# First mixer: the last two heads' projections ahead of most of the attention's; adaLN in thirds of a place, four pieces in a row

## The chip, the cores and the metric

The kernel runs on one core of a Trainium2 chip. The metric is device microseconds of one execution, from the first instruction to the last; a kernel is judged by the median of several executions. TensorE is called PE in the rows (its weight loads PEld), VectorE DVE, ScalarE ACT, GpSimd POOL, and SyncE, which only issues transfers here, SP.

## The reference, cut to what matters

A network of four layers on one sequence of 256 tokens, width 1024, in float32:

```
for layer in (0, 1):                               # first block
    mix = even_mixer(h)  if layer == 0 else  odd_mixer(h)
    h = layer_norm(a * h + mix);   h = layer_norm(a * h + conv_ffn(h))
for i in (0, 1):                                   # second block, conditioned on one vector c
    shift, scale, gate = split(silu(c) @ ada_w[i, 0] + ada_b[i, 0])       # adaLN, a "place"
    y = stick_breaking_attention(h * (1 + scale) + shift)  or  retention(...)
    h = layer_norm(a * h + (1 + gate) * y)
    shift, scale, gate = split(silu(c) @ ada_w[i, 1] + ada_b[i, 1])
    h = layer_norm(a * h + (1 + gate) * grouped_moe(h * (1 + scale) + shift))
```

`even_mixer` projects x to six heads of a gated delta rule ("DeltaNet": a causal convolution, then for each head a triangular solve and a scan over chunks of 64, gated by a projection z) and to four heads of a dilated attention (q, k, v in three groups, softmax, weights times v). `odd_mixer` projects to four heads of differential attention and four of gated linear attention (GLA). The adaLN parameters depend on c alone: four places (i, j) of 3072 numbers each, a vector of 1024 times a matrix of 1024 x 3072, 48 MB of weights in all. Nothing needs them before the second block.

## The kernel before, in words

Tokens lie as two tiles t of 128. Each projection of the first block splits weights and activations into a high and a low part and multiplies three times (`mm3`, L402 to L404). The weights come in pieces of 1 MB through a ring of six buffers; SP issues the loads (L356) in program order, each as soon as its buffer is free. PE works strictly in program order; what that order is, is decided while the program is built.

`drive` builds it: it takes one step of each active chain in turn (a chain runs in a slot; chains of one slot come one after the other) and after each the next step of a filler. In the mixers the filler is a list of items, each a generator with a condition; `work` takes the first item whose condition holds.

In `even_mixer` (items at L980 to L988) the items are `head_proj(0)`, (2), (4), which project q, k, v of two DeltaNet heads each; `swa_qk` (six) and `swa_v` (three), the attention's projections; and `z_proj(0)`, (2), (4). `z_proj(4)` waits for the flag ("pe", 0), the end of the first pair of heads. The chains are one `gdn_head` for each DeltaNet head in two slots (start L1077, inverse by levels L1151, L1158, L1159 with a masked copy L1162 on DVE, tail L1170 to L1189), eight attention units `swa_unit(h, t)` in one slot (scores L931, scale and bias L934 to L942 on DVE, softmax L819 to L821, transposes L831, weights times v L952, normalised L954), and `pair_end`, which norms and gates two heads and transposes them (L498). The attention units need all of `swa_v`. `outproj_ln` follows: L402 to L404 with 512 columns, then a layer norm whose last step is ACT L707.

The adaLN work is `ada(n)` (L1474 to L1508): n pieces of a queue of 48. A piece is one 1 MB load of 256 columns (8 row blocks), eight products of the vector with it (L1496: the vector is broadcast to 32 columns and each product goes to one of four column groups of the array), a copy to SBUF on ACT (adasb, L1502), two products with a selecting vector that sum the groups and turn the row into columns (`finish`, L1483), and two bias adds on ACT (L1486, tile adac). `N_ADA` = (18, 17, 3, 0): 18 pieces in the even mixer, one after every second item; 17 in the odd; 3 in each of three `build_xT` (transposes L423, affine L446, split L436), ahead of its first token tile; `ada(48)` (L2264) does what is left, four, ahead of the second block.

Of the kernel before, what the change touches and what calls it, by code (L numbers as in the profile page):

```python
# [15 lines left out]
AF = mybir.ActivationFunctionType  # L16
ALU = mybir.AluOpType
# [4 lines left out]
P = 128  # L22
S = 256
NT = S // P
D = 1024
KD = D // P
# [17 lines left out]
N_ADA = (18, 17, 3, 0)  # L44
# [6 lines left out]
def _consts():  # L51
    f = np.float32
    k = np.arange(P)[:, None]
    i = np.arange(P)[None, :]
    parts = {}
# [6 lines left out]
    parts["sel"] = (np.arange(P)[:, None] % 32 == 0)  # L62
    parts["MBpos"] = np.where(i <= k, 0.0, BIG)
    parts["MBneg"] = np.where(i >= k, 0.0, -BIG)
    c = np.arange(2 * P)[None, :]
# [52 lines left out]
class Net:  # L118
# [448 lines left out]
    def init_cols(self, r):  # L567


        nc = self.nc  # L570
        ps = self.bank()
# [12 lines left out]
        self.adaq = [(i, c) for i in range(4) for c in range(12)]  # L584
# [251 lines left out]
    def even_mixer(self, xn, n_ada=0):  # L836
        nc, T, tc = self.nc, self.T, self.tc
# [4 lines left out]
        with tc.tile_pool(name="em", bufs=2) as gp, self.psum_phase(c0=2, c1=2, x=1) as self.pc:  # L842
# [116 lines left out]
            def pair_end(hp):  # L959
# [18 lines left out]
            fl = self.flags  # L978
# [4 lines left out]
                *[(None, lambda i=i, b=b: swa_qk(i, b)) for b in (0, 2, 4) for i in range(2)],  # L983
                *[(None, lambda g=g: swa_v(g)) for g in range(GRP)],
                (lambda: {("go", 2), ("go", 3)} <= fl, lambda: head_proj(4)),
# [16 lines left out]
            for i in range(n_ada):  # L1002
                items.insert(4 + 2 * i, (None, lambda: self.ada(1)))
# [212 lines left out]
    def odd_mixer(self, x, xn, n_ada=0):  # L1216
# [6 lines left out]
        with tc.tile_pool(name="om", bufs=2) as op, self.psum_phase(d0=1, d1=1, g=3) as self.pc:  # L1223
# [239 lines left out]
            for i in range(n_ada):  # L1463
                items.insert(min(len(items), 3 + 2 * i), (None, lambda: self.ada(1)))
# [11 lines left out]
    def ada(self, n):  # L1476

        nc = self.nc
        prev = None

        def finish(i, c, ps, sb):
            for j in range(2):
                nc.tensor.matmul(ps[:, 256 + j : 257 + j], sb[:, j * P : j * P + P], self.sel, start=True, stop=True)  # L1483
            for j in range(2):
                dst = self.adac[:, i, 2 * c + j : 2 * c + j + 1]
                nc.scalar.activation(dst, ps[:, 256 + j : 257 + j], AF.Identity, bias=dst)  # L1486

        for _ in range(min(n, len(self.adaq))):
            i, c = self.adaq.pop(0)
            w = self.T["ada_w_2"][i // 2, i % 2].rearrange("(k p) c -> p k c", p=P)  # L1490
            wi = self.wload(w[:, :, c * 256 : c * 256 + 256], [P, KD, 256])
            wt = self.wtile(wi)
            ps = self.bank()
            for k in range(KD):
                q = (k % 4) * 32
                nc.tensor.matmul(ps[q : q + 32, :256], self.adas[:, k : k + 1].to_broadcast([P, 32]),  # L1496
                                 wt[:, k, :], start=k < 4, stop=k >= 4, tile_position=(0, q))
            yield
            if prev:
                finish(*prev)  # L1500
            sb = self.lp.tile([P, 256], F32, tag="adasb", bufs=2, name=self.nm("adasb"))
            nc.scalar.activation(sb, ps[:, :256], AF.Copy)  # L1502
            prev = (i, c, ps, sb)
            yield
        if prev:
            yield
            finish(*prev)
# [797 lines left out]
```

## Time and profile before

| | us |
|---|---|
| runs | 1894.43, 1890.86, 1882.28 |
| median of the three | 1890.86 |
| profiled execution | 1891.04 |
| its span | 1889.0 |
| PE busy in it | 1749.1 (93%) |
| even mixer, to its first output product | 0 to 282.72 |
| its output projection | 282.72 to 307.73 |
| build 1 and first FFN | 307.73 to 513.88 |
| build 2 and odd mixer with its output projection | 513.88 to 692.33 |
| build 3 and second FFN | 692.33 to about 896.7 |

Each stage ends where the next one's first PE instruction starts. In the rows of the trace a line is the start in us, the busy time, engine, line, operation, out<-in by the program's names with shapes, and in brackets how long the engine was idle ahead of it and what released it. A product in float32 is two passes, so a line's count is twice that of the program's instructions. Neighbouring products overlap, so the spacing of starts, not the busy time, is what one costs in a full stretch.

### The profile page before, as it was taken

To read this page: it belongs to the slowest core of one execution; us is meant where nothing else is said; L and a number is where in the kernel's file an instruction comes from. 1 tells how busy PE (TensorE), PEld (TensorE's weight loads), DVE (VectorE), ACT (ScalarE), POOL (GpSimd) and SP (SyncE) were. 2 spreads that over 40 slices of the span, in tenths; PEclk is the share of its full clock that TensorE was granted. 3 is DMA by queue.
4 is the path that set the end of the run, shared out by engine and by line. 5 is a ranking of instruction groups with operands and counts; after the bars stand their busy time and mean duration, and the time that the engine had idled before them with its cause. 6 is when DMAs were issued, how large, how long until landed. Compare 5 with 4: busy or idle time off the path is not lost. (4 is left out here: it accounts for less than half of the span.)

```text
span 1889.0 us, 29304 instructions
## 1 busy us (share of the span) xinstructions
PE 1749.1 (93%) x11781; PEld 1345.5 (71%) x11781; DVE 1040.1 (55%) x1963; ACT 711.4 (38%) x1346; POOL 230.5 (12%) x275
## 2 busy tenths in 40 slices
PE   7999998999989989999799799999689997999995
PEld 6989876999878869999698444433589985444432
DVE  6865854877767558777655532111477655422113
ACT  5444434555465455555565211111334332111111
POOL 2121201000043111000300010000133420100002
PEclk9999998999989989999899799999799998999998
DMA  8455554455566674556534899997344459799980
GB/s 272 149 168 164 161 175 156 157 201 197 162 212 213 210 269 157 188 172 198 186 135 166 328 401 397 401 400 265 102 149 136 155 208 348 297 402 400 403 322 24
DMA packets 275367, 434.85 MB, mean 230 GB/s; under 512 B 10549, under 2 KB 176007, under 8 KB 275093
## 3 DMA queue, kind: packets, MB, share of 16 engines
q1 hardware_dynamic: 271828, 428.49, 64.2%
q0 software_dynamic: 2016, 2.49, 0.5%
q8 instruction: 97, 1.59, 0.3%
q10 hardware_dynamic: 1377, 1.88, 0.3%
q14 instruction: 49, 0.40, 0.1%
HBM read 431.77 MB, written 1.05 MB: 229 GB/s over the span
## 5 line engine op out<-in xcount | busy, mean ns | idle before, releaser
L270 DVE TENSOR_TENSOR wl<-w,wh 128x1024 fp32r<-128x1024 f32 (+1 forms) x312 | 388.1, 1244 | 199.0 <-ACT wh L269 197.9
L269 ACT ACTIVATE wh<-w 128x1024 fp32r<-128x1024 f32 (+1 forms) x312 | 328.7, 1055 | 365.9 <-PE ps L403 175.5
L402 PE MATMUL ps<-xh,wh 128*128 128x256 f32 (+1 forms) x1312 | 384.9, 294 | 9.3 <-ACT xh L436 8.0
L403 PE MATMUL ps<-xl,wh 128*128 128x256 f32 (+1 forms) x1312 | 376.2, 287 | 0.0
L404 PE MATMUL ps<-xh,wl 128*128 128x256 f32 (+1 forms) x1312 | 375.2, 286 | 0.5 <-DVE wl L270 0.5
L402 PEld LDWEIGHTS ps<-xh,wh 128*128 128x128 f32 (+1 forms) x1312 | 253.2, 193 | 17.0 <-ACT xh L436 8.3
L403 PEld LDWEIGHTS ps<-xl,wh 128*128 128x128 f32 (+1 forms) x1312 | 253.4, 193 | 3.2 <-issue 0.8
L404 PEld LDWEIGHTS ps<-xh,wl 128*128 128x128 f32 (+1 forms) x1312 | 252.9, 193 | 2.4 <-DVE wl L270 1.0
L402 PE MATMUL ps<-wh,xh 128*128 128x256 f32 x512 | 155.6, 305 | 1.8 <-DVE rvg L728 1.4
L404 PE MATMUL ps<-wh,xl 128*128 128x256 f32 x512 | 148.3, 290 | 1.0 <-DVE xl L437 1.0
L403 PE MATMUL ps<-wl,xh 128*128 128x256 f32 x512 | 149.0, 291 | 0.0
L402 PE MATMUL pc<-wh,yh 128*128 128x512 f32 x336 | 132.1, 397 | 1.0 <-DVE yl L270 0.9
L403 PE MATMUL pc<-wl,yh 128*128 128x512 f32 x336 | 132.9, 395 | 0.0
L404 PE MATMUL pc<-wh,yl 128*128 128x512 f32 x336 | 131.6, 393 | 0.4 <-DVE yl L270 0.3
L2074 PE MATMUL pc<-w,xs 128*64 128x512 f32 x512 | 121.8, 595 | 0.0
L2074 PE MATMUL ps<-w,xs 128*64 128x512 f32 x512 | 113.3, 595 | 0.9 <-ACT pt L264 0.9
L402 PEld LDWEIGHTS ps<-wh,xh 128*128 128x128 f32 x512 | 101.5, 198 | 5.7 <-issue 2.2
L404 PEld LDWEIGHTS ps<-wh,xl 128*128 128x128 f32 x512 | 101.0, 197 | 2.0 <-DVE xl L437 1.8
L403 PEld LDWEIGHTS ps<-wl,xh 128*128 128x128 f32 x512 | 101.8, 199 | 0.4 <-issue 0.2
L2035 PEld LDWEIGHTS ps<-pe,x 128*128 128x128 f32 x576 | 70.5, 201 | 27.3 <-issue 24.3
L2074 PEld LDWEIGHTS pc<-w,xs 128*64 128x64 f32 x512 | 37.3, 137 | 72.7 <-issue 70.2
L2085 PE MATMUL ps<-w,hT 128*64 128x512 f32 x256 | 85.8, 595 | 0.0
(550 smaller groups left out, 2619.4 us busy)
## 6 DMA issues: line engine op xcount, KB each, us to landing
w<-in_moe_w_gate_dram SPq DMA_DIRECT2D x68, 1024.0 KB, 13.7
w<-in_moe_w_up_dram SPq DMA_DIRECT2D x68, 1024.0 KB, 14.7
w<-in_moe_w_down_dram SPq DMA_DIRECT2D x68, 1024.0 KB, 14.0
w<-in_ada_w_dram SPq DMA_DIRECT2D x48, 1024.0 KB, 5.9
w<-in_ffn_w_up_dram SPq DMA_DIRECT2D x44, 1024.0 KB, 5.3
w<-in_ret_w_in_dram SPq DMA_DIRECT2D x24, 1024.0 KB, 5.3
w<-in_ffn_w_down_dram SPq DMA_DIRECT2D x22, 1024.0 KB, 4.9
w<-in_w_in_even_dram SPq DMA_DIRECT2D x21, 1024.0 KB, 5.4
```

Source lines behind the costliest of these rows:

```text
L269: self.nc.scalar.activation(hi, src, AF.Copy)
L270: self.nc.vector.tensor_tensor(lo, src, hi.bitcast(F32), op=ALU.subtract)
L402: mm(ps, lh, rh, start=first, stop=False)
L403: mm(ps, lh, rl, start=False, stop=False)
L404: mm(ps, ll, rh, start=False, stop=last)
L2035: mm(ps[:, k * P : k * P + P], xn[:, t, (4 * a + k) * P : (4 * a + k + 1) * P], pef[:, t, :], start=t == 0, stop=t == 1)
L2074: mm(ps[64 * e : 64 * e + 64, :], xs[:, k, 64 * e : 64 * e + 64], wt[2 * (k // 4) + e][:, k % 4, :], start=k == 0, stop=k == KD - 1)
L2085: mm(ps[64 * e : 64 * e + 64, :], hT[:, f * P + 64 * e : f * P + 64 * e + 64], wt[2 * (f // 2) + e][:, f % 2, hf * 512 : hf * 512 + 512], ...
```

## The change

- `ada`: twelve pieces instead of 48. A piece is 1024 columns, a third of a place: four loads of 1 MB in a row (two row blocks of 1024 columns each, so that a row of a block is 4 KB in one run instead of 1 KB), 32 products (each row block against the four column quarters; quarter q goes to column group q), one copy of 128 x 256 to SBUF, two products with a selecting matrix of four columns, two adds on DVE. The products L1496 stay 384 and the bytes 48 MB; copies go from 48 to 12, finishing products from 96 to 24, adds from 96 on ACT to 24 on DVE.
- `N_ADA` = (4, 4, 1, 0): 16 MB in the even mixer (18 before), 16 in the odd (17), 4 in each build (3), 4 at the end (4).
- Even mixer: the four pieces stand behind all other items instead of between them. Since `z_proj(4)` waits for its flag, they come ahead of it.
- Odd mixer: a piece after every seventh item instead of every second; the last two follow all projections.
- `head_proj(4)` moves from behind `swa_v` to behind the first two `swa_qk`, with its old condition.

```diff
-N_ADA = (18, 17, 3, 0)
+N_ADA = (4, 4, 1, 0)
-    parts["sel"] = (np.arange(P)[:, None] % 32 == 0)
+    parts["sel"] = (k == 32 * np.arange(4)[None, :])
-        self.adaq = [(i, c) for i in range(4) for c in range(12)]
+        self.adaq = [(i, c) for i in range(4) for c in range(3)]
-                *[(None, lambda i=i, b=b: swa_qk(i, b)) for b in (0, 2, 4) for i in range(2)],
+                (None, lambda: swa_qk(0, 0)),
+                (None, lambda: swa_qk(1, 0)),
+                (lambda: {("go", 2), ("go", 3)} <= fl, lambda: head_proj(4)),
+                *[(None, lambda i=i, b=b: swa_qk(i, b)) for b in (2, 4) for i in range(2)],
                 *[(None, lambda g=g: swa_v(g)) for g in range(GRP)],
-                (lambda: {("go", 2), ("go", 3)} <= fl, lambda: head_proj(4)),
-                items.insert(4 + 2 * i, (None, lambda: self.ada(1)))
+                items.insert(len(items) - i, (None, lambda: self.ada(1)))
-                items.insert(min(len(items), 3 + 2 * i), (None, lambda: self.ada(1)))
+                items.insert(min(len(items), 3 + 7 * i), (None, lambda: self.ada(1)))
     def ada(self, n):
-            wi = self.wload(w[:, :, c * 256 : c * 256 + 256], [P, KD, 256])
+            ws = [self.wload(w[:, k : k + 2, c * D : c * D + D], [P, 2, D]) for k in range(0, KD, 2)]
             ps = self.bank()
             for k in range(KD):
-                q = (k % 4) * 32
-                nc.tensor.matmul(ps[q : q + 32, :256], self.adas[:, k : k + 1].to_broadcast([P, 32]),
-                                 wt[:, k, :], start=k < 4, stop=k >= 4, tile_position=(0, q))
+                for q in range(0, P, 32):
+                    nc.tensor.matmul(ps[q : q + 32, :256], self.adas[:, k : k + 1].to_broadcast([P, 32]),
+                                     self.wtile(ws[k // 2])[:, k % 2, 8 * q : 8 * q + 256],
+                                     start=k == 0, stop=k == KD - 1, tile_position=(0, q))
             yield
-            if prev:
-                finish(*prev)
             sb = self.lp.tile([P, 256], F32, tag="adasb", bufs=2, name=self.nm("adasb"))
             nc.scalar.activation(sb, ps[:, :256], AF.Copy)
-            prev = (i, c, ps, sb)
             yield
-        if prev:
             yield
-            finish(*prev)
+            for j in range(2):
+                nc.tensor.matmul(ps[:, 256 + 4 * j : 260 + 4 * j], sb[:, j * P : j * P + P], self.sel,
+                                 start=True, stop=True)
+            for j in range(2):
+                dst = self.adac[:, i, 8 * c + j : 8 * c + 8 : 2]
+                nc.vector.tensor_tensor(dst, ps[:, 256 + 4 * j : 260 + 4 * j], dst, op=ALU.add)
```

How the instructions now stand, at three places. First PE in the last part of the even mixer, from the last projection product of `z_proj(4)` on (gD and gW are the inverse of a DeltaNet head, ident,sc the attention's transposes, vb,spT its weights times v, w,adacc an adaLN product). Before, it begins:

```order
L404 MATMUL ps_2873<-wh_2697,xl_116 128x256
L1496 MATMUL ps_2976<-w_2742,adacc 32x256 x8
L1151 MATMUL pc_2987<-gD_2464,gna_2425 128x128 x2
L1151 MATMUL pc_2992<-gD_2765,gna_2710 128x128 x2
L1483 MATMUL ps_2976<-cst_171,adasb_2985 128x1 x2
L1496 MATMUL ps_3003<-w_2777,adacc 32x256 x8
L831 MATMUL pc_3013<-ident,sc_2860 128x128 x4
```

and after the change, from the first complete unit of tile 1 in it:

```order
L498 MATMUL ps_3013<-ident,gon_2019 128x128
L498 MATMUL ps_3020<-ident,gon_2019 128x128
L931 MATMUL pc_3028<-kb,qb 128x256 x2
L931 MATMUL pc_3032<-kb,qb 128x256
L831 MATMUL pc_3042<-ident,sc_3027 128x128 x4
L831 MATMUL pc_3048<-ident,sc_3027 128x128 x2
L952 MATMUL pc_3052<-vb,spT_3041 128x64 x6
L931 MATMUL pc_3065<-kb,qb 128x128 x3
```

Where the end of two heads and three adaLN pieces stood between the attention's instructions, the attention's instructions now follow one another. Behind the last projection there were 40 DeltaNet products, two and a half attention units, and three adaLN pieces; now there are 9 DeltaNet products, four units and a half, and 26 products of the adaLN piece of build 1, which belong to the last unit's waits.

Second, SP's loads ahead of that. Before, adaLN and projection weights alternate:

```order
L356 DMA w_1285<-in_ada_w_dram 128x8x256
L356 DMA w_1393<-in_w_in_even_dram 128x8x256
L356 DMA w_1424<-in_ada_w_dram 128x8x256
L356 DMA w_1538<-in_w_in_even_dram 128x8x256
L356 DMA w_1582<-in_ada_w_dram 128x8x256
```

and now sixteen adaLN loads stand in a row, of which these are the first with the last projection piece ahead of them:

```order
L356 DMA w_1517<-in_w_in_even_dram 128x8x256
L356 DMA w_1879<-in_ada_w_dram 128x2x1024
L356 DMA w_1978<-in_ada_w_dram 128x2x1024
L356 DMA w_2082<-in_ada_w_dram 128x2x1024
L356 DMA w_2189<-in_ada_w_dram 128x2x1024
L356 DMA w_2303<-in_ada_w_dram 128x2x1024
```

Only the weights of `z_proj(4)` and of the output projection come behind them.

Third, PE at the end of the odd mixer (glq,glk are the GLA scores of the last level, glv,gla_kn its state, gla_at its weights, gla_st,gla_qe the state's part of the output, ident,oo transposes of the heads' outputs). Before, from the last projection products on:

```order
L402 MATMUL ps_7065<-wh_6936,xh_5632 128x256
L403 MATMUL ps_7065<-wl_6937,xh_5632 128x256
L404 MATMUL ps_7065<-wh_6936,xl_5633 128x256
L1496 MATMUL ps_7159<-w_6818,adacc 32x256 x8
L1400 MATMUL pc_7174<-glv,gla_at 128x128
L1403 MATMUL pc_7174<-gla_st,gla_qe 128x128
```

and after the change, from the second adaLN piece behind the last projection on:

```order
L1489 MATMUL ps_6943<-w_6779,adacc 32x256 x8
L1444 MATMUL pc_6990<-dfv,dpT_6924 128x128
L1444 MATMUL pc_6999<-dfv,dpT_6929 128x128 x2
L1498 MATMUL ps_6943<-cst_171,adasb_6988 128x4 x2
L1365 MATMUL pc_7005<-glq,glk 128x128
L1365 MATMUL pc_7006<-glq,glk 128x128
```

The last projection product stood four heads' final GLA products ahead of the mixer's end, with seven adaLN pieces around and behind them; now it stands ahead of the last two levels of the GLA scores (L1365, before L1363), the state (L1391), all its outputs, and two adaLN pieces.

## Rows read from the trace of the kernel before

**Rows 1.** The page: span, and the adaLN loads (KB each, median us to landing).

```profile
span 1889.0 us, 29304 instructions
...
w<-in_ada_w_dram SPq DMA_DIRECT2D x48, 1024.0 KB, 5.9
```

**Rows 2.** PE in order of time, end of the last projection of the even mixer.

```profile
254.21 0.28 PE L404 MATMUL ps<-wh,xl 128*128 128x256 f32 x1
254.42 1.07 PE L1496 MATMUL ps<-w,adacc 128*32 128x256 f32 x16
255.42 1.16 PE L1151 MATMUL pc<-gD,gna 128*128 128x128 f32 x8
256.42 0.50 PE L1483 MATMUL ps<-cst,adasb 128*128 128x1 f32 x4
256.85 1.07 PE L1496 MATMUL ps<-w,adacc 128*32 128x256 f32 x16
```

**Rows 3.** PE in order of time, the attention's last units before the output projection.

```profile
263.21 1.45 PE L952 MATMUL pc<-vb,spT 128*128 128x64 f32 x12
...
265.99 0.93 PE L931 MATMUL pc<-kb,qb 64*128 64x128 f32 x6
...
270.90 0.79 PE L952 MATMUL pc<-vb,spT 128*128 128x64 f32 x6
...
272.23 1.13 PE L931 MATMUL pc<-kb,qb 64*128 64x256 f32 x4
...
277.79 0.60 PE L831 MATMUL pc<-ident,sc 128*128 128x128 f32 x4
...
280.09 2.12 PE L952 MATMUL pc<-vb,spT 128*128 128x64 f32 x12 [0.52 <-DVE spT L266]
...
282.72 0.77 PE L402 MATMUL pc<-wh,yh 128*128 128x512 f32 x1
```

**Rows 4.** Windows: PE, PEld, DVE, ACT, POOL busy (instructions), PEclk, DMA share, GB/s.

```profile
254.00:265.00 11.00, 11.00 (x120) 9.08 (x118) 5.69 (x12) 5.75 (x18) 0.00 (x0) 1.00 1.01 346
...
270.00:275.00 5.00, 4.62 (x28) 3.29 (x25) 2.70 (x9) 0.49 (x1) 0.00 (x0) 1.00 0.00 0
275.00:280.00 5.00, 2.97 (x18) 1.99 (x17) 2.88 (x9) 2.53 (x8) 0.00 (x0) 1.00 0.00 0
280.00:285.00 5.00, 4.53 (x21) 3.86 (x22) 2.65 (x10) 0.39 (x1) 1.03 (x1) 0.59 0.00 0
```

**Rows 5.** PE in order of time, build 1 up to the first FFN product.

```profile
307.73 1.93 PE L1496 MATMUL ps<-w,adacc 128*32 128x256 f32 x32
...
312.29 0.55 PE L423 MATMUL ps<-ident,x 128*128 128x128 f32 x3 [1.09 <-ACT adac L1486]
...
323.11 0.93 PE L402 MATMUL ps<-xh,wh 128*128 128x256 f32 x2 [4.26 <-ACT xh L436]
```

**Rows 6.** ACT in order of time, the layer norm's last step ahead of build 1.

```profile
307.24 0.81 ACT L707 ACTIVATE x<-lnt,lnrs 128x512 f32<-128x512 f32 x1 [6.74 <-POOL lnrs L687]
...
311.12 0.81 ACT L707 ACTIVATE x<-lnt,lnrs 128x512 f32<-128x512 f32 x1 [1.88 <-POOL lnrs L687]
```

**Rows 7.** PE in order of time, builds 2 and 3.

```profile
521.00 0.66 PE L423 MATMUL ps<-ident,x 128*128 128x128 f32 x4 [0.71 <-ACT adac L1486]
...
692.33 1.93 PE L1496 MATMUL ps<-w,adacc 128*32 128x256 f32 x32
...
696.90 0.55 PE L423 MATMUL ps<-ident,x 128*128 128x128 f32 x3 [1.10 <-ACT adac L1486]
```

**Rows 8.** PE in order of time, the end of the odd mixer's projections and its output projection.

```profile
649.64 0.28 PE L404 MATMUL ps<-wh,xl 128*128 128x256 f32 x1
...
652.52 0.39 PE L1403 MATMUL pc<-gla_st,gla_qe 128*128 128x128 f32 x2
...
670.60 0.66 PE L498 MATMUL ps<-ident,oo 128*128 128x128 f32 x4
```

**Rows 9.** POOL in order of time, the last gate of the odd mixer.

```profile
660.80 1.27 POOL L1211 TENSOR_TENSOR oo<-oo,glr 128x512 f32<-128x512 f32 x1 [0.75 <-DVE oo L1208]
```

More of the change, by code (lines that the diff above doesn't have):

```diff
@@ L1478, in ada @@
         nc = self.nc
[L1479 to L1486, printed above, removed]
         for _ in range(min(n, len(self.adaq))):
@@ L1490, in ada @@
             w = self.T["ada_w_2"][i // 2, i % 2].rearrange("(k p) c -> p k c", p=P)
-            wi = self.wload(w[:, :, c * 256 : c * 256 + 256], [P, KD, 256])
-            wt = self.wtile(wi)
+            ws = [self.wload(w[:, k : k + 2, c * D : c * D + D], [P, 2, D]) for k in range(0, KD, 2)]
             ps = self.bank()
             for k in range(KD):
-                q = (k % 4) * 32
-                nc.tensor.matmul(ps[q : q + 32, :256], self.adas[:, k : k + 1].to_broadcast([P, 32]),
-                                 wt[:, k, :], start=k < 4, stop=k >= 4, tile_position=(0, q))
+                for q in range(0, P, 32):
+                    nc.tensor.matmul(ps[q : q + 32, :256], self.adas[:, k : k + 1].to_broadcast([P, 32]),
+                                     self.wtile(ws[k // 2])[:, k % 2, 8 * q : 8 * q + 256],
+                                     start=k == 0, stop=k == KD - 1, tile_position=(0, q))
             yield
-            if prev:
-                finish(*prev)
             sb = self.lp.tile([P, 256], F32, tag="adasb", bufs=2, name=self.nm("adasb"))
             nc.scalar.activation(sb, ps[:, :256], AF.Copy)
-            prev = (i, c, ps, sb)
             yield
-        if prev:
             yield
-            finish(*prev)
+            for j in range(2):
[4 more added lines that the diff above has]
+                nc.vector.tensor_tensor(dst, ps[:, 256 + 4 * j : 260 + 4 * j], dst, op=ALU.add)
     def ada_gate(self, pool, i):
```

## The prediction, made before the changed kernel had run

> **What bounds the kernel now.** I read the page first: the span is 1889.0 us [rows 1], the profiled execution took 1891.04 us, 0.2 us above the median of the runs; 2 us of it lie outside the span. PE is busy in nearly all of it (the table above). So a PE instruction taken out of a full stretch is worth its spacing, and one taken out of a wait is worth nothing; the question for each edit is which of the two stretches it lies in. I then read PE in order of time at the places that the change touches.
>
> The even mixer is full up to the last product of `z_proj(4)` at 254.21, and in that stretch an adaLN piece costs PE 1.00 us for its eight products (254.42 to 255.42, where the next line starts) and 0.43 us for its finish (256.42 to 256.85) [rows 2]. From there to the first output product at 282.72 the attention sets the pace: its last two units run one after the other, tile 0 of head 3 from 265.99 and tile 1 from 272.23 [rows 3]. The windows show PE 4.62 of 5 us busy at 270 to 275 and 2.97 at 275 to 280, both at the full clock (2.4 GHz), and 0.59 in the slice after, where the clock has gone down to its lower level (1.2 GHz) [rows 4]. That tail, 28.3 us, is what the new order makes longer or shorter.
>
> At the builds PE waits on the adaLN work itself: the first transpose of build 1 is released by ACT adac at 312.29, 4.6 us after the output projection ended, and build 3's at 696.90, 4.6 us after 692.33 [rows 5, 7]. At the odd mixer's end adaLN pieces stand behind the last projection (649.64), and the last head outputs are transposed only at 670.60, although their last gate on POOL ended at 660.80 + 1.27 = 662.07 [rows 8, 9].
>
> **The even mixer up to the end of the projections.** Taken out ahead of `z_proj(4)`'s end: fifteen finishes at 0.43 = 6.5 us. Put in: four finishes of the new form, two instructions with four columns instead of one; no row has that form, so between the old price, 0.43, and one main piece, 1.00; I take 0.45, nearest to the row with the same weights, = 1.8 us. One more MB of products (16 against 15 ahead of that point): 1.0. The heads 4 and 5 start earlier, so 31 of the 40 DeltaNet products that stood behind the projections now stand ahead, at 0.22 to 0.25 each (the four of L1151 in rows 2 take 255.42 to 256.42): 6.9. In return 4.2 us of attention products and transposes move behind. Sum -6.5 + 1.8 + 1.0 + 6.9 - 4.2 = -1.0: the projections end at about 253.4. The copies and adds taken off ACT and the 24 adds put on DVE lie beside full PE work and are costed at nothing; without that cover a piece's two adds would cost no more than its old finish, 0.43, 1.7 us for the four here.
>
> **The tail, the largest term.** Before, it held the end of two heads, three adaLN pieces and two and a half attention units; now nearly nothing but four and a half units, one after another in one slot. A tile-0 unit takes from 265.99 to 270.90 + 0.79 = 271.7, 5.7 us, of which a head's work on ACT and PE costs some 0.2: 5.5. A tile-1 unit takes from 272.23 to 280.09 + 2.12 = 282.2, 10.0; its last group took 2.12 us at the low clock where the same group took 1.45 at the full one, so 9.3 at the full clock. The half unit that is left from head 1 runs from the transposes (277.79) to its end, 4.4 there, 3.8 to 4.0 at the full clock [rows 3]. So 4.0 + 5.5 + 9.3 + 5.5 + 9.3 = 33.6, and 0.5 + 0.5 for the transposes of the last attention output and of the last pair of heads: the output projection starts at 253.4 + 34.6 = 288.0, **5.3 us later** than 282.72, if the clock stays up. It did not in the tail of before, which was fuller. The three last units have 4.2 + 2.3 + 4.2 = 10.7 us of PE work on their chain (a tile-1 unit 1.13 for its first scores, half of that for the rest, 0.60 for four transposes, 0.30 to 0.40 for two, 1.45; a tile-0 unit 0.93, some 0.5 for three transposes, 0.79); at the measured ratio 2.12/1.45 the low clock adds 0.46 of it, 5 us, and at double time 10.7. I take **6**, near the measured ratio. The 26 adaLN products of build 1 that now stand there (3.5 us) lie inside the last unit's wait for the softmax, in which PE was idle for 2 us [rows 4]. The term is then 5.3 + 6 = **+11.3**, bounds +4 (full clock, units 0.3 faster each) and +18 (double time, heads 4 and 5 late by 2).
>
> The row says that the clock still read 1.00 in a slice with 2.97 of 5 us busy, and 0.59 in the next [rows 4]; by the first alone the term is +5.3 and the time 1886, by the second +11.3 and 1892. The Trainium skill, "TensorE: Matmul & The Clock Gate", section "HAM oscillation — how this bites in real kernels", says that a kernel whose bursts of products are shorter than the waits between them falls to the low clock and starts each next burst cold; by that rule the longer tail is the second case, and the trace of before agrees as far as its one drop goes.
>
> **The loads.** Sixteen adaLN loads in a row pass the one ring of six buffers that all weights use; behind them on SP wait `z_proj(4)`'s weights and the four of the output projection. By the order PE uses the last ten of them over about 31 us, one per 3 us. At 346 GB/s, the rate in a slice with the queues full [rows 4], 1 MB takes 3.0 us: they come just ahead, and I cost them at nothing. The other bound is below, in the rivals.
>
> **Build 1 and 3.** The pieces' products are done in the tail but for six (0.8 us), so the transposes of tile 0 start at about 308.6 instead of 312.29 (x of tile 0 is ready at 307.24 + 0.81). Tile 1 can't start before 311.12 + 0.81 = 311.9 [rows 5, 6], where half of before's transposes stood at 314.1 and later: a gain between 2.2 and 3.7, taken as **-3**. In build 3 the 32 products (4.3 us) stay, three finish groups and the waits for adac go: **-1.5** (0 to -2). In build 2 the transposes' wait of 0.71 for adac goes and two finishes: **-1** (0 to -2) [rows 7]. The last four pieces, at 897, lie behind a layer norm before and after: 0.
>
> **The odd mixer.** Of its 17 pieces ten stood ahead of the last projection: 10 x 1.43 = 14.3 us; now two pieces of 4 MB do, 2 x (4.0 + 0.45) = 8.9, and the GLA scores, state and transposes that now follow were another 6 us ahead: the last projection ends about 11.5 us earlier, near 638.3. Behind it stand two pieces (8.9 us) and the GLA's last two levels, state and outputs, some 18 us of PE work with waits, to about 656 to 659; before, those outputs ended at 652.5 and the last transposes followed 18 us later [rows 8]. The chain from the outputs to the gate is 662.07 - 652.9 = 9.2 us [rows 9], so the last transposes come at about 666, 4.6 us earlier than 670.60; the output projection runs behind them as before: **-5** (-2 with the chain exposed for longer, -8 without a wait).
>
> **Sum.** 1891.04 + 11.3 - 3 - 1 - 1.5 - 5 = 1891.8, **1892 us**. All of the second block is unchanged.
>
> **Rivals.** (a) The clock stays up in the tail: the adaLN products and the last head fill it enough. For it: 1.00 at 2.97 of 5 busy; against it: the drop at 280 in a fuller tail. 1891.8 - 6 = 1886. (b) The removed PE work comes through in full, because the attention's units overlap with what is ahead of them and the tail stays 28.3 us: then the projections' 1 us, three builds and the odd mixer's best give 1891 - 1 - 3.7 - 2 - 2 - 8 = 1874. Against it: the units share one slot and one score buffer. (c) Slower: the adaLN loads are late, PE waits for each in order, and the projections behind them with it. The page's median landing is 5.9 us [rows 1]; one after the other the last ten loads would take 59 us where PE uses 31: +28, 1920. It decides from 3.1 us a load on; at 3.6, +5 and 1897; at 5, +19 and 1911. For it: the ring has no other work between; against it: 346 GB/s with the same ring. (d) The change does not show: the tail's loss and the other gains cancel; that is the forecast itself.
>
> **How the numbers follow.** About 1% (19 us) is what a measurement of this kernel can tell from no change; the three runs of before lie 12 us apart. Forecast (1887 to 1898) 0.48; (a), 1880 to 1887, 0.22; (b), down to 1870, 0.13; (c) 0.17, of which half ends above 1904. Taking a tenth at each end leaves **1875 to 1904**. Faster by over 1% (below 1872) is the lower half of (b), 0.07; slower by over 1% (above 1910) the far part of (c), 0.07; same 0.86.
>
> **What would show it.** In the profile after: the last `z_proj(4)` product near 253 and the first output product near 294 (a: 288; b: 282 or earlier; c: waits of PE for a load of ada_w ahead of 253); a granted clock of 0.5 to 0.6 in the windows from about 265 on; the first transpose of build 1 within 1.5 us of the output projection's end; the last odd projection near 638 after taking off the mixer's later start. I would be wrong above all if the tail's units ran faster or slower one by one than the two that I read, or if the heads 4 and 5 moved ahead made PE wait for the masked copies there.

## The result and the profile after

The changed kernel takes 1903.95 us (median of six runs, 1901.46 to 1909.52) against 1890.76 in the same comparison: a ratio of 1.0086 with a 95% interval of 1.0069 to 1.0103. It is slower, by 13.2 us as the medians lie and by 16 as the ratio has it. The forecast was 1892, no change, in a range whose top, 1904, the time reaches.

The page of the kernel after, with PE's granted clock over the span in the last line:

```profile
span 1907.8 us, 28868 instructions
...
PE 1746.8 (92%) x11637; PEld 1345.2 (71%) x11637; DVE 1039.9 (55%) x1987; ACT 680.0 (36%) x1214; POOL 227.5 (12%) x275
...
PEclk9999978999989989999899899999789998999998
```

PE's busy time fell by only 2.3 us (1749.1 before) although 144 passes of finishing products are gone. Products at the low clock are busy for nearly twice as long (2.82 us against 1.45, below), and there are more of them: slices 6 and 7 of the forty read 7 and 8, where before they read 9 and 8.

Where the time went in the two profiled executions. A stage ends where the next one's first PE instruction starts; the projections end with their last product:

| stage | before | after | longer by |
|---|---|---|---|
| to the end of the even mixer's projections | 254.5 | 249.9 | -4.6 |
| from there to the first output product (the tail) | 28.2 | 46.8 | +18.6 |
| output projection, even | 25.0 | 22.2 | -2.8 |
| build 1, to the first FFN product | 15.4 | 15.3 | -0.1 |
| first FFN | 190.8 | 189.9 | -0.9 |
| build 2 and odd mixer to the last projection | 136.0 | 126.8 | -9.3 |
| from there to the end of the odd output projection | 42.4 | 52.2 | +9.8 |
| build 3 | 14.9 | 15.2 | +0.3 |

At build 3's end this execution is 11.0 us behind, at the second block's first transpose 12.2. It is the longest of its six: it loses another 6.6 us in the second block, which is the same in all kernels here and takes 977 to 987 us in their profiled executions, 987 in this one.

The tail, PE in order of time (these answer to [rows 3]):

```profile
249.63 0.29 PE L404 MATMUL ps<-wh,xl 128*128 128x256 f32 x1
...
259.55 0.55 PE L831 MATMUL pc<-ident,sc 128*128 128x128 f32 x3 [1.98 <-ACT sc L820]
...
263.43 2.07 PE L931 MATMUL pc<-kb,qb 64*128 64x256 f32 x4
266.29 1.22 PE L931 MATMUL pc<-kb,qb 64*128 64x256 f32 x2 [0.78 <-DVE sc L937]
270.13 1.12 PE L831 MATMUL pc<-ident,sc 128*128 128x128 f32 x4 [2.62 <-ACT sc L820]
...
273.25 2.82 PE L952 MATMUL pc<-vb,spT 128*128 128x64 f32 x12 [0.53 <-ACT spT L264]
276.45 1.65 PE L931 MATMUL pc<-kb,qb 64*128 64x128 f32 x6 [0.38 <-DVE swo L954]
...
283.68 2.07 PE L931 MATMUL pc<-kb,qb 64*128 64x256 f32 x4 [0.38 <-DVE swo L954]
...
286.09 1.91 PE L1489 MATMUL ps<-w,adacc 128*32 128x256 f32 x10
287.93 1.22 PE L931 MATMUL pc<-kb,qb 64*128 64x256 f32 x2
289.08 3.32 PE L1489 MATMUL ps<-w,adacc 128*32 128x256 f32 x38
292.33 0.66 PE L831 MATMUL pc<-ident,sc 128*128 128x128 f32 x4
...
296.75 0.48 PE L402 MATMUL pc<-wh,yh 128*128 128x512 f32 x1
```

One attention unit follows the other with little between them, and each waits for the softmax and then for the copies. Tile 1 of head 2 takes from 263.43 to 273.25 + 2.82 = 276.1, 12.6 us; tile 0 of head 3 from 276.45 to 283.3, 6.8. The group of twelve took 2.82 us where it took 1.45 at the full clock [rows 3]. The windows say why (PE, PEld, DVE, ACT, POOL busy, PEclk, DMA share, GB/s):

```profile
250.00:260.00 10.00, 6.86 (x47) 5.30 (x45) 5.38 (x14) 3.87 (x11) 0.83 (x2) 1.00 0.31 106
260.00:270.00 10.00, 6.14 (x19) 4.08 (x18) 5.40 (x14) 2.38 (x6) 2.11 (x4) 0.52 0.00 0
270.00:280.00 10.00, 6.27 (x24) 4.99 (x24) 2.25 (x5) 1.01 (x4) 0.20 (x1) 0.50 0.00 1
280.00:290.00 10.00, 8.77 (x38) 4.72 (x42) 2.48 (x6) 0.15 (x2) 0.00 (x0) 0.50 0.01 2
```

In 250 to 260 PE is busy 6.86 of 10 us at the full clock; from about 261 to 291 the clock is at its low level, 1.2 GHz.

### The profile page after: what moved, and what is told of

Same layout as the page of the kernel before. It is cut to its first block, busy times and chain, and to the rows that moved or that the text cites. A ratio compares the mean times of both kernels' runs of the same rounds, so it can differ in the third digit from the quotient of the medians.

```text
span 1907.8 us, 28868 instructions
## 1 busy us (share of the span) xinstructions
PE 1746.8 (92%) x11637; PEld 1345.2 (71%) x11637; DVE 1039.9 (55%) x1987; ACT 680.0 (36%) x1214; POOL 227.5 (12%) x275
## 5 line engine op out<-in xcount | busy, mean ns | idle before, releaser
L402 PEld LDWEIGHTS ps<-xh,wh 128*128 128x128 f32 (+1 forms) x1312 | 254.5, 194 | 17.0 <-ACT xh L436 8.4
```

The lines of the kernel that those rows point to most:

```text
L402: mm(ps, lh, rh, start=first, stop=False)
```

## The experiments

Two things were open: what made the even mixer's tail longer (the move of the heads, the coarse pieces, their place, or the clock), and why the odd mixer and the builds gave nothing back. The runs are best read in one table: the first attention score, the end of the projections, how many pairs of attention units (a tile 0 and a tile 1) are left behind it, counted by their transposes, nine to a pair, and the first output product. Times in us from one profiled execution each, medians and ratios from all runs.

| run | first score | projections end | pairs left | output starts | tail | median | ratio to before (95%) |
|---|---|---|---|---|---|---|---|
| before | 176.0 | 254.5 | 1.7 | 282.7 | 28.2 | 1890.8 | |
| after | 183.8 | 249.9 | 2.7 | 296.8 | 46.8 | 1904.0 | 1.0086 (1.0069 to 1.0103) |
| odd_spread | 185.5 | 251.5 | 2.7 | 301.8 | 50.2 | 1905.6 | 1.0066 (1.0046 to 1.0086) |
| heads_late | 159.1 | 252.6 | 2.0 | 292.9 | 40.3 | 1897.0 | 1.0026 (1.0008 to 1.0043) |
| ada_spread | 204.5 | 236.4 | 3.7 | 303.6 | 67.2 | 1911.1 | 1.0106 (1.0067 to 1.0145) |
| move_only | 215.0 | 246.5 | 3.0 | 319.5 | 73.0 | 1923.5 | 1.0173 (1.0137 to 1.0210) |
| ada_only | 172.0 | 239.8 | 2.7 | 290.6 | 50.9 | 1891.3 | 0.9996 (0.9984 to 1.0008) |
| fine_steps | 175.4 | 247.0 | 2.0 | 285.9 | 38.8 | 1886.1 | 0.9964 (0.9950 to 0.9978) |
| att_ahead | 176.5 | 253.4 | 1.0 | 274.1 | 20.7 | 1879.8 | 0.9942 (0.9926 to 0.9959) |
| late_att_ahead | 165.8 | 258.5 | 0.7 | 276.4 | 17.9 | 1882.9 | 0.9955 (0.9941 to 0.9969) |
| att_gla_ahead | 176.4 | 253.9 | 1.0 | 274.5 | 20.7 | 1878.7 | 0.9934 (0.9918 to 0.9951) |

after and odd_spread have the same PE instructions in the same order up to the first output product, and reach it at 296.8 and 301.8. So a single start can differ by 5 us with nothing changed; the pairs that are left come from the order, and what a change is worth is read from the medians and ratios.

### The parts of the change

heads_late undoes the move alone:

```diff
-                (lambda: {("go", 2), ("go", 3)} <= fl, lambda: head_proj(4)),
                 *[(None, lambda i=i, b=b: swa_qk(i, b)) for b in (2, 4) for i in range(2)],
                 *[(None, lambda g=g: swa_v(g)) for g in range(GRP)],
+                (lambda: {("go", 2), ("go", 3)} <= fl, lambda: head_proj(4)),
```

> The changed kernel with head_proj(4) put back behind swa_v; the new adaLN pieces stay, at their new places. Theory (the move of the heads empties the tail: two attention units fewer lie ahead of the last projection): the tail behind the last projection has two pairs of attention units instead of two and two thirds, 26 DeltaNet products instead of 9; the output projection starts 5 to 10 us earlier than in the changed kernel (296.75), the time is 1894 to 1899. Rival (the coarse adaLN pieces are the cause, whatever the order of the heads): within 2 us of 1904. Second rival (the low clock sets the tail, and any tail without projections falls to it): the tail is shorter only by the one unit, 9 to 13 us.

Measured: 1897.03, the output projection 3.9 us earlier, the tail 6.6 us shorter. The move costs about 7 us beside the new pieces, as the first theory had it in the time (1894 to 1899); the output projection's start moved by less than its 5 to 10. But heads_late is still slower than before by 0.26%: the move is not all.

ada_spread undoes only the place of the even mixer's pieces:

```diff
-                items.insert(len(items) - i, (None, lambda: self.ada(1)))
+                items.insert(4 + 5 * i, (None, lambda: self.ada(1)))
```

> The changed kernel with the even mixer's four adaLN pieces after every fifth item instead of behind all items; heads and odd mixer as changed. Theory (what stands between the attention's steps sets how far the attention has come when the projections end): without the pieces at the end the attention has fewer steps there, the tail gets a third more units (3.7 pairs of units instead of 2.7), the projections end 5 us earlier, the sum is 8 to 15 us slower: 1911 to 1919. Rival (sixteen loads and four pieces in a row are what costs, PE waits for loads or for the finish): faster, 1895 or below.

Measured: 1911.09, slower still by the medians; the intervals of the two overlap (1.0067 to 1.0145 against 1.0069 to 1.0103), so by how much isn't settled. Four pieces in a row did not cost anything by themselves: on the line of the adaLN products PE waited 1.0 us in all, three times, for a load of ada_w in the whole execution of after, and the attention had a stretch to run in. So by the medians the place at the end made up for part of the move.

move_only is the kernel before with the heads moved, 48 pieces as they were.

> The kernel before with head_proj(4) moved as in the change; adaLN in 48 pieces at its old places. Theory (the move empties the tail): three pairs of attention units in the tail instead of 1.7, but eight adaLN pieces among them; 5 to 12 us slower than before, 1896 to 1903. Rival (the coarse pieces are the cause): within 2 us of 1891.

Measured: 1923.49, 32 us slower, much more than either theory said. The first score comes 39 us later (215.0 against 176.0), because the move puts the projections of two heads ahead of `swa_v`, for which every attention unit waits; three pairs are left. The pieces placed at the end in the change take away what stood ahead of `swa_v` and bring the first score back to 183.8. The change is two moves against each other, and the sum is what was measured. The two don't simply add: with the heads late the pieces behind all items are slower by some 6 us than spread ones (heads_late 1897.0, ada_only below 1891.3; the odd mixer's places differ as well).

ada_only takes the new pieces alone, heads as before (the edit of heads_late), pieces spread in both mixers:

```diff
-                items.insert(len(items) - i, (None, lambda: self.ada(1)))
+                items.insert(4 + 5 * i, (None, lambda: self.ada(1)))
-                items.insert(min(len(items), 3 + 7 * i), (None, lambda: self.ada(1)))
+                items.insert(min(len(items), 3 + 4 * i), (None, lambda: self.ada(1)))
```

> The new adaLN pieces alone, as near to the old places as four pieces can be: after every fifth item in the even mixer, after every fourth in the odd, heads as before. Rival (PE is nearly always busy, so the 36 finishes come through): 1875 to 1880. Theory (the coarse pieces give the filler fewer steps, so that the chains are left behind): 2.7 pairs of attention units and 56 DeltaNet products in the even mixer's tail; the projections end 15 us earlier and the output projection starts later than before all the same, 285 to 295; 1890 to 1900.

Measured: 1891.33, ratio 0.9996: nothing, with PE busy for 12.5 us less (1736.6 against 1749.1). PE in order of time shows the even mixer's part of it going into the tail:

```profile
239.51 0.28 PE L404 MATMUL ps<-wh,xl 128*128 128x256 f32 x1
...
290.63 0.48 PE L402 MATMUL pc<-wh,yh 128*128 128x512 f32 x1
```

The projections end 14.7 us earlier than before, and the output projection starts 7.9 us later. The PE work that was removed had been the filler between the attention's steps.

### The step, not the size

fine_steps is ada_only with more yields and nothing else (in every adaLN piece):

```diff
                                      start=k == 0, stop=k == KD - 1, tile_position=(0, q))
-            yield
+                if k % 2 == 1:
+                    yield
```

> The run ada_only with a filler step (a yield) after every two row blocks of an adaLN piece instead of after all eight, so that a piece of 4 MB gives the chains three steps more. Same products, loads and places. Theory (what a round of the chains gets to fill with is a step, whatever its size; few large steps leave the chains behind): two pairs of attention units in the tail instead of 2.7; the output projection starts 4 to 9 us earlier than in ada_only (290.63), the time is 1882 to 1888. Rival (the tail depends on what PE has left to do, not on how it is cut): within 2 us of 1891.

Measured: 1886.10, within the theory's 1882 to 1888 and clear of ada_only (0.9950 to 0.9978 against 0.9984 to 1.0008). The output projection starts 4.7 us earlier than in ada_only, the projections end 7.3 us later. No product, load or place differs, only the number of steps: behind each step of a chain `drive` takes one filler step, so what the attention gets done ahead of the projections' end goes by the number of filler steps. A piece of 1 MB gave three steps for 1.4 us of PE; a piece of 4 MB gives three for 4.4.

### The attention ahead

att_steps (the changed kernel, heads late) and before_att_steps (the kernel before) leave out the filler step behind each attention step:

```diff
-            self.drive(self.work(items), chains, per=1)
+            self.drive(self.work(items), chains, per=lambda c: int(c.slot != "x"))
```

> The changed kernel with head_proj(4) back behind swa_v, and with no filler step behind a step of the attention's chain (per of drive is 0 for slot x, 1 for the others). The attention then takes a step after every two or three filler steps instead of after every three or four. Theory (how many attention units are left when the projections end sets the tail): no unit is left behind the last projection, the tail holds only 32 adaLN products and 8 of DeltaNet; the output projection starts at 268 to 276 instead of 296.75, the time is 1872 to 1883. Rival (steps closer together make PE wait for DVE and ACT ahead of the last projection instead): the projections end 5 to 15 us later, the time is 1885 to 1897.

> The kernel before with only the attention's chain changed as in the run att_steps; 48 adaLN pieces, heads and places as before. Theory: no attention unit in the tail, 27 DeltaNet products and five adaLN pieces left; the output projection starts at 273 to 279 instead of 282.72, the time is 1882 to 1888; what att_steps is faster than this, 8 to 12 us, is what the coarse pieces are worth in PE work (18 finishes here against 4, and the odd mixer's). Rival (as there): 1890 or above.

Measured: 1940.04 and 1949.00, 2.6% and 3.0% slower. Neither theory held as it stood. In the stretch in which no DeltaNet head was active, the attention was the only chain, and the rule then gave no filler at all: the attention ran nearly alone from 168 on, soon at the low clock (windows of att_steps):

```profile
180.00:200.00 20.00, 12.39 (x40) 8.67 (x40) 4.63 (x10) 2.61 (x6) 2.09 (x3) 0.50 0.00 0
200.00:220.00 20.00, 12.33 (x40) 8.69 (x40) 4.83 (x11) 2.71 (x7) 2.09 (x3) 0.50 0.00 0
```

Useful as a price: one pair of units, alone and at the low clock, takes 20 us; the two windows hold 40 PE instructions each, the same work twice.

att_ahead mends that. It is ada_only with this rule, so that a filler step stands behind an attention step whenever no head runs:

```diff
-            self.drive(self.work(items), chains, per=1)
+            self.drive(self.work(items), chains, per=lambda c: int(c.slot != "x" or not any(("go", h) in fl and ("gdn", h) not in fl for h in range(H))))
```

> The run ada_only with no filler step behind an attention step while a DeltaNet head is active (one behind it, as before, when none is; the run att_steps had left it out there too, and with that all filler). Theory (the attention units that are left when the projections end set the tail): one pair of units and 34 DeltaNet products in the tail instead of 2.7 and 56; the output projection starts at 272 to 282 instead of 290.63, the time is 1873 to 1884. Rival (closer steps make PE wait ahead of the projections' end by as much): 1887 to 1893.

Measured: 1879.80, within the first theory's 1873 to 1884; the output projection starts at 274.1, 16.6 us earlier than in ada_only, of which 11.5 are left in the time. No run has this rule with the 48 old pieces, so how much of the 11 us under the kernel before needs the coarse pieces isn't shown. The tail is 20.7 us, and the clock stays up in it (windows of att_ahead):

```profile
250.00:260.00 10.00, 9.48 (x79) 8.81 (x78) 7.97 (x17) 5.46 (x16) 0.00 (x0) 1.00 0.34 108
260.00:270.00 10.00, 8.25 (x49) 6.06 (x49) 5.46 (x12) 2.39 (x5) 0.00 (x0) 1.00 0.00 1
270.00:280.00 10.00, 7.83 (x45) 6.16 (x45) 4.58 (x15) 2.77 (x8) 1.02 (x1) 1.00 0.01 2
```

late_att_ahead has the same rule with the four pieces behind all items, as the change puts them (heads late, the odd mixer's pieces after every fourth item).

> The changed kernel with head_proj(4) back behind swa_v, the filler rule of att_ahead, and the odd mixer's pieces after every fourth item: the four adaLN pieces of the even mixer stay behind all items. Theory: two thirds of a pair of units, 14 DeltaNet products and 32 adaLN products in the tail; the output projection starts at 270 to 280, the time is 1872 to 1882, 1 to 4 us under att_ahead since the adaLN work fills the tail's waits. Rival (adaLN loads in a row stop PE): above att_ahead.

Measured: 1882.87. Its tail is the shortest of the table, 17.9 us, but its projections end 5.1 us later than att_ahead's. It isn't under att_ahead, as the theory had it; the intervals of the two overlap, so which place is better isn't settled.

### The clock in the tail

warm_tail is the changed kernel with transposes of the identity in each unit's wait for the softmax, once the last projection is placed:

```diff
                 r = self.softmax_rows(sc[:, : GRP * nk])
+                if ("z", 4) in self.flags:
+                    for j in range(10 * (t + 1)):
+                        nc.tensor.transpose(ps[:, j % 4 * P : j % 4 * P + P], self.ident, self.ident)
                 yield
```

> The changed kernel with idle work on PE in the tail of the even mixer: behind the scores of each attention unit that starts after the last projection stand 10 (tile 0) or 20 (tile 1) transposes of the identity into the unit's own, already read bank, some 1.2 and 2.4 us at the full clock, in the wait for the softmax. Their result is used by nothing. Theory (the low clock makes up a third of the tail): the granted clock stays at 1.0, the tail falls from 47 to 36 to 40 us, the time is 1893 to 1898. Rival (the waits for DVE and ACT set the tail, the clock nothing): within 2 us of 1904, or slower by up to 6 where the transposes stand in the way.

Measured: 1906.70, ratio 1.0085 (1.0068 to 1.0101), as after's. The clock was higher in the tail, but the time is no shorter (windows and PE of warm_tail):

```profile
260.00:270.00 10.00, 7.16 (x49) 5.53 (x48) 5.93 (x19) 2.87 (x10) 1.04 (x1) 1.00 0.00 0
270.00:280.00 10.00, 7.64 (x44) 6.42 (x45) 2.73 (x6) 1.41 (x3) 2.11 (x3) 0.83 0.01 2
280.00:290.00 10.00, 8.10 (x39) 5.22 (x39) 2.81 (x6) 0.71 (x2) 0.00 (x0) 0.72 0.00 0
```

```profile
268.03 1.13 PE L931 MATMUL pc<-kb,qb 64*128 64x256 f32 x4
...
271.15 3.89 PE L947 MATMUL pc<-ident 128*128 128x128 f32 x20 [0.52 <-DVE sc L942]
275.19 0.63 PE L831 MATMUL pc<-ident,sc 128*128 128x128 f32 x4
...
277.58 1.55 PE L955 MATMUL pc<-vb,spT 128*128 128x64 f32 x12 [0.53 <-ACT spT L264]
```

Tile 1 of head 2 takes 268.03 to 279.1, 11.1 us against 12.6 in after, although its idle transposes took 3.89 us instead of 2.4: the clock was down to 0.50 from 271 to 274 and came up again in the middle of them. The tail is 47.4 us against 46.8. So the low clock costs at least 1.5 us in a tile-1 unit, and this run can't say how much more: the idle work stood in the way of the units that it kept warm. In att_ahead, where fewer units are left and 34 DeltaNet products stand among them, the clock stayed up without such work.

### The odd mixer

odd_spread moves the changed kernel's odd pieces ahead of the last projection:

```diff
-                items.insert(min(len(items), 3 + 7 * i), (None, lambda: self.ada(1)))
+                items.insert(min(len(items), 3 + 4 * i), (None, lambda: self.ada(1)))
```

> The changed kernel with the odd mixer's four adaLN pieces after every fourth item instead of every seventh: all four ahead of the last projection. Theory (behind the odd mixer's last projection the GLA's levels, state and outputs are a chain of waits, and two pieces of PE work lie in its shadow; moved ahead they cost their full 9 us there): the last projection ends 5 to 9 us later, its tail of 52 us shrinks by about as much or less: 1902 to 1909. Rival (the pieces behind the last projection delay the chain): 3 to 6 us faster, 1898 to 1901.

Measured: 1905.63, which can't be told from after. From the end of the first FFN to the end of the odd output projection it takes 177.8 us against 179.0 in after (178.5 before): the two pieces behind the last projection cost little or nothing there, as the theory said, and moving them gains nothing that the times show.

att_gla_ahead is att_ahead with one filler step behind a GLA step:

```diff
-            self.drive(self.work(items), chains, per=lambda c: 1 + (c.slot == "g"))
+            self.drive(self.work(items), chains, per=1)
```

> The run att_ahead, and in the odd mixer one filler step behind a step of the GLA chain instead of two. The order shows four transposes between the last projection and the output projection instead of the GLA's last level, state and outputs. Theory (that chain behind the last projection is what ate the odd mixer's saving): the odd mixer from the end of the first FFN to its output projection's end takes 164 to 172 us instead of 176, the time is 6 to 12 us under att_ahead. Rival (the chain's waits on POOL and DVE move ahead with it and stop PE there): within 2 us of att_ahead, or slower.

Measured: 1878.70, 1.1 us lower, well inside the intervals of both: the rival's outcome, not the theory's 6 to 12. That stretch takes 173.5 us against 177.2 in att_ahead, but that shows no gain: late_att_ahead has att_ahead's PE order there, instruction for instruction, and takes 173.0 (ada_only and odd_spread have it too, 175.5 and 177.8). The windows of that stretch in att_ahead and late_att_ahead read the same work at a granted clock of 0.92 and 0.95:

```profile
502.99:680.19 177.20, 158.32 (x1311) 137.43 (x1310) 113.86 (x207) 79.12 (x175) 48.63 (x54) 0.92 0.63 223
...
506.01:679.03 173.02, 154.40 (x1311) 132.67 (x1310) 113.14 (x207) 79.02 (x175) 48.86 (x54) 0.95 0.65 229
```

The GLA's chain did move ahead of the last projection, which then ended 7.8 us later; with the chain PE's idle time moved there (16.6 us ahead of the last projection's end and 3.2 behind it, 12.0 and 6.9 in att_ahead), as the rival said. It is the lowest median measured, 0.66% under the kernel before and 1.3% under the change, and not to be told from att_ahead.

## Why the prediction was right or wrong

**The tail: right in kind and sign, too small.** The forecast put the whole loss there, +11.3 with bounds +4 and +18; the output projection started 14.0 us later. The projections ended at 249.9 instead of 253.4. Of these 3.5 us, 2.3 are in one of the five small sums: two attention units moved behind the projections, by the forecast's own prices 2.3 + 4.2 = 6.5 us of PE work, and the sum has 4.2. The rest, 1.2, is within what one execution can differ: odd_spread, with the same order, ends them at 251.5. The tail itself took 46.8 us where the forecast has 34.6 + 6. A tile-1 unit took 12.6 us where 9.3 and its share of the low clock make 11.2, a tile-0 unit 6.8 to 7.1 where 5.5 and its share make 6.5. By the busy times of their groups at the two levels the low clock cost some 7.6 us, an estimate, 3.6 of it in the one tile-1 unit that lay wholly in it; the forecast had 6. The measured ratio it was sized by, 2.12/1.45, was of a group that the clock had covered only in part (it read 0.95 from 280 to 281 and 0.50 after); the same group at the low clock throughout took 2.82. And PE stands 1.2 us ahead of tile 1 of head 2, in the transposes of the last pair of heads, which the forecast counted only at the end. The 26 adaLN products of build 1, put at nothing, stand in front of the last unit's second scores and transposes, which come 1.4 and 0.6 us later there than in the tile-1 unit before it.

Rival (a), the clock staying up, was wrong: bursts with waits between them stayed at the low clock from about 261 to 291. The clock fell once and stayed down, while PE was busy for 6.1 to 8.8 of 10 us. The Trainium skill's rule in "TensorE: Matmul & The Clock Gate", section "HAM oscillation — how this bites in real kernels", agreed with the trace in kind.

**What was not forecast: the output projection 2.8 us shorter.** Before, its first products ran at the low clock, 0.63 to 0.78 us each, with transposes of the last heads among them; after, PE was busy without a wait from 286 on, the adaLN products among its work, the clock came up at 291, and the products take 0.40 from the second on.

**The step that failed: the gains counted behind the tail.** Against the tail's loss the forecast set 10.5 us: -3, -1 and -1.5 at the three builds and -5 in the odd mixer. Build 1 gave 0.1, build 2 and the odd mixer together lost 0.5, build 3 lost 0.3. With the output projection's 2.8 and the FFN's 0.9 that is why 14.0 us of loss were still 11.0 at build 3's end where 0.8 was forecast.

**The builds.** The forecast let transposes start earlier and counted that as time. Build 1's first transposes did start at once, 319.96, 1.0 us after the output projection ended (4.6 before), but what they feed stands behind the layer norm's last step on ACT and DVE, and that came later (ACT and DVE of after):

```profile
323.15 0.81 ACT L707 ACTIVATE x<-lnt,lnrs 128x512 f32<-128x512 f32 x1 [2.69 <-DVE lnada L597]
...
324.81 0.78 ACT L446 ACTIVATE bx<-ps,lnc 128x128 f32<-128x128 f32 x2
```

```profile
319.80 0.69 DVE L638 BATCH_NORM_STATS2 lnst<-lnt 128x6 f32<-128x512 f32 x1
321.23 0.16 DVE L1502 TENSOR_TENSOR adac<-ps,adac 128x4 f32<-128x4 f32 x1 [0.73 <-PE ps L1498]
321.31 0.20 DVE L651 BATCH_NORM_AGGREGATE lnmv<-lnst 128x2 f32<-128x12 f32 x1
...
324.00 0.73 DVE L448 TENSOR_SCALAR bx<-ps,lnc 128x128 f32<-128x128 f32 x2 [0.86 <-ACT x L707]
```

The same affine step (L448, which scales the transposed columns) in before:

```profile
313.45 0.41 DVE L448 TENSOR_SCALAR bx<-ps,lnc 128x128 f32<-128x128 f32 x1 [2.41 <-PE ps L423]
```

It came 1.5 us after x of tile 1 was ready at 311.93 [rows 6], so by these rows earlier transposes could give 1.5 and not 3. And the adds moved from ACT to DVE now stand in DVE's order between the layer norm's statistics and their aggregate (L651), and wait 0.73 us for PE's finish: x of tile 1 is ready 5.0 us after the output projection ended, 4.2 before. So the affine step came 0.7 us earlier after the output projection's end, and the first FFN product 0.1. The prediction had asked what the adds cost beside full PE work and not what is queued behind them on DVE at the builds. In build 3 tile 0's transposes came early as well, but the finish (L1498) waits 1.74 us for the copy (L1494), which now stands behind the layer norm's last step and two weight splits in ACT's order, and tile 1's transposes wait for the finish: +0.3 (ACT of after):

```profile
706.50 0.82 ACT L707 ACTIVATE x<-lnt,lnrs 128x512 f32<-128x512 f32 x1 [3.02 <-POOL lnrs L687]
707.22 1.99 ACT L269 ACTIVATE wh<-w 128x1024 fp32r<-128x1024 f32 x2
709.11 0.36 ACT L1494 ACTIVATE adasb<-ps 128x256 f32<-128x256 f32 x1
```

**The odd mixer: the work came off, and idle time took its place.** Relative to the first FFN's end the last projection came 9.3 us earlier (11.5 forecast, and 1 in build 2), and the tail behind it took 9.8 more. PE and POOL of after (they answer to [rows 8, 9]):

```profile
650.63 0.28 PE L404 MATMUL ps<-wh,xl 128*128 128x256 f32 x1
...
672.89 0.39 PE L1405 MATMUL pc<-gla_st,gla_qe 128*128 128x128 f32 x2
...
684.15 0.38 PE L498 MATMUL ps<-ident,oo 128*128 128x128 f32 x2
```

```profile
680.85 1.28 POOL L1213 TENSOR_TENSOR oo<-oo,glr 128x512 f32<-128x512 f32 x1 [0.76 <-DVE oo L1210]
```

The GLA's outputs end 22.4 us behind the last projection, where 18 to 21 had been forecast and 3.0 stood before; the chain to the gate is 8.9 us, as forecast (9.2). The reading that the last transposes of before stood at 670.60 is wrong: one more group of them follows, at 672.72. Against that one the last transposes end 1 us later than before, relative to the FFN, where the forecast's 666 would have been 6.7 earlier. From the first FFN's end to the end of the odd output projection the windows of before and after read (PE, PEld, DVE, ACT, POOL busy, PEclk, DMA share, GB/s):

```profile
513.88:692.33 178.45, 165.53 (x1372) 139.36 (x1371) 112.48 (x197) 91.41 (x230) 50.07 (x54) 0.94 0.69 222
...
524.15:703.10 178.95, 160.19 (x1311) 137.80 (x1311) 114.55 (x207) 78.40 (x175) 47.29 (x54) 0.91 0.63 221
```

PE was busy for 5.3 us less and idle for 5.8 more, 4.5 of it behind the last projection. The forecast saw the exposed chain, mis-sized its waits (at most 3 us in its 18 to 21), and counted the removed filler as time all the same. This holds in the other profiled executions: PE idles for 13 to 14 us of this stretch in the three with the old pieces and for 18 to 21 in the eleven with the coarse ones, wherever the pieces and the GLA's chain stand in it.

**The loads: right, and rivals (b) and (c) did not come in.** Sixteen loads in a row came ahead of their use, at 391 to 410 GB/s in the windows from 210 to 240, against (c). The removed PE work shows nowhere by itself, against (b), as ada_only says most plainly.

**What the forecast did not see at all** is that the change removes filler steps. It took the new order from the program and read it rightly, but as a result of the move; the runs show the move, the place and the step as three effects on one quantity, how far the attention has come when the projections end. Beside the other parts of the change the move is worth about +7 (heads_late against after) and the place about -7 by the medians (after against ada_spread); in ada_only the fewer steps cost all that the removed finishes would have brought.

## What to carry to other kernels

Where PE is busy 93% of the time because independent work fills the waits of latency-bound chains, removing some of that work, or cutting it into fewer and larger steps, may gain nothing by itself, as here: count how many chain steps are left when the filler ends, and price them alone and at the low clock. Letting the chains advance more per filler step is what gained here (ada_only to att_ahead, 11.5 us); whether the filler work was then worth removing isn't shown. And an instruction moved to a less busy engine has to be looked at in that engine's order: what stands behind it, and whether that is what the next stage waits for.

## What the runs showed of the hardware

At the low clock the attention's groups took nearly twice their time (2.82 us against 1.45), and with its waits a pair of units took 20 us alone. In after the clock stood at 0.50 from about 261 to 291; it fell after PE had waited 1.98 us for the softmax at 257.6 and come back to short groups. In att_ahead it stayed at 1.00 through the whole tail. The same PE instructions in the same order took 173.0 to 177.8 us in four executions (the odd mixer of late_att_ahead, ada_only, att_ahead and odd_spread), at a granted clock of 0.95, 0.94, 0.92 and 0.92; so a stage's time in one execution is good to some us only. Not expected: the profiled execution of after loses 6.6 us against before's in the second block, which is the same in both (12.2 us behind at its first transpose, 18.8 at its end), while the medians lie 13.2 us apart.
